# A two-layer streaming encoder: Newton's iteration for the Delta net's norms in three parts, and the input's norm in program order, scaled by parts

## The chip, the cores and the metric

The kernel runs on one core of one Trainium2 chip. The metric is device time in microseconds (us) of one execution; the time before is 2560.07 us, the median of 3 runs (2559.36 to 2560.88). The core's engines run side by side, each through its own list of instructions in order: TensorE (PE, matmuls and transposes), VectorE (DVE), ScalarE (ACT), GpSimd (POOL) and SyncE (SP, which issues most transfers). They wait for each other by semaphores.

## The reference

An input `x` of 1024 positions by 1024 channels goes through a layer of gated Delta net (linear attention by chunks), a gated FFN with a short convolution, a layer of banded softmax attention, a second FFN and a final norm. All of it is in float32. What the change touches is the first layer and the norm in front of it:

```python
def rmsnorm(x, g):
    y = xf * lax.rsqrt(jnp.mean(xf * xf, axis=-1, keepdims=True) + EPS)
    return (y * g.astype(jnp.float32)).astype(x.dtype)

def _l2norm(t):
    return t * lax.rsqrt(jnp.sum(t * t, axis=-1, keepdims=True) + EPS)

def gated_deltanet(xn, ...):
    proj = xn @ w_in
    qkv = silu(causal_dwconv(proj[..., :A_CONV_WIDTH], conv_w))      # 4 taps
    q = _l2norm(q heads) * A_HEAD_K ** -0.5      # 8 heads of 128
    k = _l2norm(k heads)
    ...
    o = chunk_gated_delta_rule(q, k, v, beta, g)
    o = rmsnorm(o, out_norm_w) * silu(z)
    return o @ w_out
```

So there are three reciprocal square roots in this stage: the input's norm over 1024 channels, the norms of q and k over 128, and the norm of the output over 128.

## The kernel before, in words

**Matmuls.** A float32 product is made from three passes in a faster 32-bit format: each operand is cut into a high half (ACT rounds it) and a low half (the difference, on DVE or POOL), and high x high, low x high and high x low are added in PSUM (`dense`, L113, its three matmuls at L119 to L121). Activations are `xh` and `xl` (8 k tiles of 128 channels, two halves `s` of 512 positions); a weight tile of 128 columns is cut by `split_w` (L91) into `whi` (ACT, L102) and `wlo` (POOL, L104, in four pieces).

**The start** (`begin_input`, L1227). Eight tiles of `x`, 128 positions each, are loaded (`take_x`), and two weight tiles, in this order on SP's queue: x tiles 0 to 3, the two weight tiles, x tiles 4 to 7. `norm_x` (L1150) makes for each x tile the sum of squares (ACT, L1154), its root (ACT, L1155), the reciprocal (DVE, L1156) and the scaling of the tile's 1024 channels in place (DVE, L1157). `turn_x` (L1159) transposes for each k tile four x tiles on TensorE into one PSUM tile `pxt` (L1163), from which ACT makes `xh` (L1164) and DVE `xl` (L1165). Three k tiles of the first half are turned, then the first projection tile begins, one k tile at a time, with the next transposes between. In this part only PE's order is written out by hand; on the other engines the framework's scheduler orders the instructions. Everything under `tc.manual_schedule(engines=...)` keeps, on those engines, the order in which the program records it.

**The Delta net stage.** Here PE, DVE and ACT are all recorded by hand, by a planner (`Flow`, L199). It holds generators, each with a rank and a lock (one item of a lock at a time), and a model time `T`. `wv.on("D", c)` books `c` us on its model of DVE and returns the time at which the work will be done; a generator that yields a time is taken up again half a microsecond (`slack`) after it, and one that yields nothing is taken up again after half a microsecond from the present. Between items the planner records one k tile's three matmuls of the dense stream (projections of q, k, v and z, later the output projection), 0.69 us of its time each. What it records stands in that order on PE, DVE and ACT; POOL and SP follow the scheduler. Among its items:

- `project` (L667): the convolution's taps on DVE (L682, L686), read from the PSUM tile `acc`, which is free again only then; SiLU on ACT (L691) and POOL (L692, L693).
- `gram(t)` (L738), four times, for four heads and half of the positions: the decay mask (L752), the Gram matrix on PE (L778), the norms' sums and the masked matrix on DVE (L783 to L790); at the end one `rsqrt` for all four heads, and the mark `scale`, for which `prep` waits. All calls of `gram` share a lock, so the next starts when one has ended.
- `invert_blocks` (L852): a solve of blocks of 16 on DVE, column by column (L869, L870).
- `merge` and `chain` (L891, L979): the triangular inverse, and the recurrence over chunks, in small matmuls on PE (L912 to L953; L993, L997, L1006), each of which waits for a short operation of DVE or ACT (L995, L1002, L1012).
- `finish(t, j)` (L1020), eight times, for two heads: the output's and q's norms in one factor by `rsqrt`, a scaling on POOL (L1043), and transposes.
- `yz`, `turn_last` (L1107, L1093): the gate, and the activations of the output projection (L1125, L1130); `out_tile` (L1311) is the output projection itself.

`rsqrt` (L604) is a reciprocal square root by bits on DVE: a shift and a subtraction for a first value (L607, L608), then three times Newton's step in three instructions (L610 to L612), 11 instructions on 16 or 8 numbers per partition.

Of the kernel before, what the change touches and what calls it, by code (L numbers as in the profile page):

```python
# [13 lines left out]
ALU = mybir.AluOpType  # L14
AX = mybir.AxisListType

P = 128
SEQ = 1024
# [10 lines left out]
def trunk_kernel(  # L29
# [15 lines left out]
    nc = tc.nc  # L45
# [394 lines left out]
    wv = None  # L440
# [130 lines left out]
    with ExitStack() as ph:  # L571
# [19 lines left out]
        def gt(name):  # L591
            return dp.tile([P, 8, 8], F32, name=name, tag=name)

        beta, gg, t1, t2 = gt("beta"), gt("gg"), gt("t1"), gt("t2")
# [9 lines left out]
        def rsqrt(y, a, w):  # L604

            yi = y.bitcast(I32)
            nc.vector.tensor_scalar(yi, a.bitcast(I32), 1, None, op0=ALU.logical_shift_right)  # L607
            nc.vector.tensor_scalar(yi, yi, -1, 0x5F3759DF, op0=ALU.mult, op1=ALU.add)  # L608
            for _ in range(3):
                nc.vector.tensor_tensor(w, y, y, op=ALU.mult)  # L610
                nc.vector.scalar_tensor_tensor(w, w, -0.5, a, op0=ALU.mult, op1=ALU.mult)
                nc.vector.scalar_tensor_tensor(y, w, 1.5, y, op0=ALU.add, op1=ALU.mult)  # L612

        ssk, ssq, sk, ck, nck = gt("ssk"), gt("ssq"), gt("sk"), gt("ck"), gt("nck")
        soo, ff, rr = gg, gt("ff"), gt("rr")
# [18 lines left out]
        def raw_tile(c0):  # L634
            raw = wp.tile([P, KT, P], F32, name="wraw", tag="wraw", bufs=2)
            nc.sync.dma_start(out=raw, in_=a_w_in[:, c0 : c0 + P].rearrange("(k p) m -> p k m", p=P))
            return raw
# [69 lines left out]
        def cs(c):  # L707
            return slice(c * P, (c + 1) * P)
# [3 lines left out]
        def heads(t):  # L712

            return t // 2, range(4 * (t % 2), 4 * (t % 2) + 4)
# [23 lines left out]
        def gram(t):  # L738

            s, hds = heads(t)  # L740
            Es, fetched = [], []
            sl = slice(4 * s, 4 * s + 4)
            h4 = slice(hds[0], hds[0] + 4)

            def fetch(hd):
                fetched.append(wv.T)
                Es.append(dq.tile([P, 4, P], F32, name="E", tag="E", bufs=3))
                nc.sync.dma_start(out=Es[-1], in_=d_g[sl, hd, :].rearrange("(o c) t -> o c t", o=1).broadcast_to([P, 4, P]))

            def decay(i):  # L750
                hd, E = hds[i], Es[i]
                nc.vector.tensor_tensor(E, E, negm.rearrange("p (o t) -> p o t", o=1).broadcast_to([P, 4, P]), op=ALU.add)  # L752
                yield wv.on("D", 0.8) - wv.slack
                for c in range(4):
                    nc.scalar.activation(E[:, c], E[:, c], AF.Exp, bias=ngc[:, 4 * s + c, hd : hd + 1])
                nc.sync.dma_start(out=d_e[hd][s], in_=E)
                stored[hd, s] = wv.T + 5.0
                yield wv.on("A", 1.45)

            fetch(hds[0])  # L760
            fetch(hds[1])
            yield wv.T + 5.5
            for i, hd in enumerate(hds):
                need = [("k", hd, 0) if s == 0 else ("in", hd)]
                if t > 1:
                    need.append(("merged", hd, s - 1))
                need = wv.when(*need)
                while need() is None:
                    yield wv.T + 0.5
                yield need()  # L770
                if i < 2:
                    fetch(hds[i + 2])
                yield from decay(i)
                slot = yield from wv.bank()
                pg = paux.tile([P, 4, P], F32, name="pg", tag="pa")
                kq, E = kqs[hd, s], Es[i]
                for c in range(4):
                    mm(pg[:, c], kq[:, 0, cs(c)], kq[:, 0, cs(c)], start=True, stop=True)  # L778
                wv.pe(4)
                h1 = slice(hd, hd + 1)  # L780
                mn = dq.tile([P, 4, P], F32, name="mn", tag="mn", bufs=8)
                for c in range(4):
                    nc.vector.tensor_tensor_reduce(out=mn[:, c], in0=pg[:, c], in1=ident, op0=ALU.mult, op1=ALU.add, scale=1.0, scalar=0.0, accum_out=ssk[:, 4 * s + c, h1])  # L783
                nc.vector.tensor_scalar(ssk[:, sl, h1], ssk[:, sl, h1], EPS, None, op0=ALU.add)
                nc.vector.reciprocal(t1[:, sl, h1], ssk[:, sl, h1])
                nc.vector.tensor_tensor(ck[:, sl, h1], t1[:, sl, h1], beta[:, sl, h1], op=ALU.mult)
                nc.vector.tensor_scalar(nck[:, sl, h1], ck[:, sl, h1], -1.0, None, op0=ALU.mult)
                wv.on("D", 1.95)
                for c in range(4):
                    nc.vector.scalar_tensor_tensor(mn[:, c], pg[:, c], nck[:, 4 * s + c, h1], E[:, c], op0=ALU.mult, op1=ALU.mult)  # L790
                slot[0] = t_ = wv.on("D", 1.2)
                yield t_ - wv.slack
                cm = dq.tile([P, 4, 32], F32, name="cm", tag="cm", bufs=2)
                for b in range(4):
                    r = slice(32 * b, 32 * b + 32)
                    nc.gpsimd.tensor_copy(cm[r], mn[r, :, r])
                nc.sync.dma_start(out=d_ms[t][i].rearrange("c b j i -> (b j) c i"), in_=cm)
                mns[hd, s] = mn
                wv.mark(("gram", hd, s), wv.on("G", 1.2, t_) + 2.5)
                yield max(wv.T + 0.5, fetched[min(i + 1, 3)] + 5.5)  # L800
            rsqrt(sk[:, sl, h4], ssk[:, sl, h4], t2[:, sl, h4])
            nc.vector.tensor_tensor(sk[:, sl, h4], sk[:, sl, h4], ssk[:, sl, h4], op=ALU.mult)
            wv.mark(("scale", t), wv.on("D", 3.5))

        def prep(hd, s):

# [213 lines left out]
        def finish(t, j):  # L1020

            s, hds = heads(t)
            hds = hds[2 * j : 2 * j + 2]
            sl = slice(4 * s, 4 * s + 4)
            h2 = slice(hds[0], hds[0] + 2)
            vvs = [parts[hd, s][2] for hd in hds]
            for hd, vv in zip(hds, vvs):
                junk = dp.tile([P, P], F32, name="junk2", tag="junk", bufs=1)
                for c in range(4):
                    nc.scalar.activation(junk, vv[:, c], AF.Square, accum_out=soo[:, 4 * s + c, hd : hd + 1])  # L1030
                t_ = wv.on("A", 1.9)
                yield
            yield t_ - wv.slack
            f = ff[:, sl, h2]
            nc.vector.tensor_scalar(f, ssq[:, sl, h2], EPS, 128.0 * EPS, op0=ALU.add, op1=ALU.mult)
            nc.vector.scalar_tensor_tensor(f, soo[:, sl, h2], 1.0 / 128.0, f, op0=ALU.mult, op1=ALU.add)
            r = rr[:, sl, h2]
            rsqrt(r, f, t2[:, sl, h2])
            t_ = wv.on("D", 3.6)
            yield t_ - wv.slack  # L1040
            for hd, vv in zip(hds, vvs):
                fa = rr[:, sl, hd : hd + 1].broadcast_to([P, 4, P])
                nc.gpsimd.tensor_tensor(vv, vv, fa, op=ALU.mult)  # L1043
                t_ = wv.on("G", 1.1, t_)
            yield t_
            for hd, vv in zip(hds, vvs):
                yield from (turn if t < 3 else turn_last)(hd, s, vv)
# [96 lines left out]
        def take_x(i):  # L1144

            t_ = dp.tile([P, 2, HALF + 4], F32, name="xt", tag="kq", bufs=8)
            x_tiles.append(t_.rearrange("p j t -> p (j t)")[:, 0:SEQ])
            nc.sync.dma_start(out=x_tiles[i], in_=x[i * P : (i + 1) * P, :])

        def norm_x(i):  # L1150
            t_ = x_tiles[i]
            jk = dp.tile([P, 8, P], F32, name="xj", tag="U", bufs=2).rearrange("p c t -> p (c t)")
            r = dp.tile([P, 2], F32, name="rsx", tag="rsx", bufs=4)
            nc.scalar.activation(jk, t_, AF.Square, accum_out=r[:, 0:1])  # L1154
            nc.scalar.activation(r[:, 1:2], r[:, 0:1], AF.Sqrt, scale=1.0 / SEQ, bias=epst)  # L1155
            nc.vector.reciprocal(r[:, 1:2], r[:, 1:2])  # L1156
            nc.vector.tensor_scalar(t_, t_, r[:, 1:2], None, op0=ALU.mult)  # L1157

        def turn_x(s):  # L1159
            for k in range(KT):  # L1160
# [66 lines left out]
        def begin_input():  # L1227
# [2 lines left out]
            nc.scalar.activation(warm[:, 0:1], epst, AF.Sqrt)  # L1230
            for i in range(4):
                take_x(i)
            for i in range(4):
                norm_x(i)
            raws = [raw_tile(m * P) for m in (8, 9)]
            wts = [split_w(raws[0], [P, KT, P])]
            for i in range(4, 8):
# [116 lines left out]
        wv = Flow()  # L1354
# [664 lines left out]
    with ExitStack() as ph:  # L2019
# [102 lines left out]
        def attend(a, tp, kv, sc, oT, more, tail):  # L2122
# [63 lines left out]
            def end():  # L2186
                last()
                finish()
# [70 lines left out]
        wv = Weave()  # L2259
# [104 lines left out]
    ctx_f, _ = ffn(1, h, hp, normed, tails[0], d_r1, norm_out)  # L2364
# [58 lines left out]
```

## Time and profile before

| | before |
|---|---|
| median of 3 runs | 2560.07 us |
| profiled execution | 2559.29 us |
| its span, first to last instruction | 2557.6 us |
| granted TensorE clock, mean | 0.999 |
| TensorE busy | 2498.8 us (98%) |
| VectorE busy | 1858.0 us (73%) |
| ScalarE busy | 1415.2 us (55%) |
| GpSimd busy | 1464.4 us (57%) |

In rows of the timeline the columns are start, duration (both us), engine, line, operation, output and inputs, and how many instructions the row merges; in brackets stands the engine's idle time before it and what ended it. Durations of matmuls are modelled ends; the distance of their starts tells the pace. In rows of waits stand the waiting engine, tile and line, what it waited for, the total in us, how often, and the longest.

### The profile page before, as it was taken

To read this page: it belongs to the slowest core of one execution; us is meant where nothing else is said; L and a number is where in the kernel's file an instruction comes from. 1 tells how busy PE (TensorE), PEld (TensorE's weight loads), DVE (VectorE), ACT (ScalarE), POOL (GpSimd) and SP (SyncE) were. 2 spreads that over 40 slices of the span, in tenths; PEclk is the share of its full clock that TensorE was granted. 3 is DMA by queue.
4 is the path that set the end of the run, shared out by engine and by line. 5 is a ranking of instruction groups with operands and counts; after the bars stand their busy time and mean duration, and the time that the engine had idled before them with its cause. 6 is when DMAs were issued, how large, how long until landed. Compare 5 with 4: busy or idle time off the path is not lost.

```text
span 2557.6 us, 39388 instructions
## 1 busy us (share of the span) xinstructions
PE 2498.8 (98%) x13933; PEld 2065.6 (81%) x13933; DVE 1858.0 (73%) x3109; ACT 1415.2 (55%) x2736; POOL 1464.4 (57%) x1460
## 2 busy tenths in 40 slices
PE   7999999999999999999999999999999999999999
PEld 5878888888877888888778888888876788888877
DVE  4775775554688888888876666667488788888886
ACT  5444555464455655555556565556455655556554
POOL 3655553445347777777726444443433777777771
PEclk9999999999999999999999999999999999999999
DMA  4433445464337777777831211113332567677786
GB/s 128 138 106 117 125 128 153 144 190 148 104 87 146 147 145 154 155 148 159 197 131 54 66 52 57 44 51 101 100 102 79 136 143 152 142 154 154 154 183 212
DMA packets 320598, 325.15 MB, mean 127 GB/s; under 512 B 32912, under 2 KB 244624, under 8 KB 320400
## 3 DMA queue, kind: packets, MB, share of 16 engines
q1 hardware_dynamic: 289440, 219.33, 29.1%
q0 software_dynamic: 25920, 94.38, 20.8%
q10 hardware_dynamic: 5040, 8.91, 1.0%
q8 instruction: 110, 1.80, 0.3%
q14 instruction: 88, 0.72, 0.1%
HBM read 179.89 MB, written 142.67 MB: 126 GB/s over the span
## 4 chain that ended last, share of the span: by engine, by line
PE 56%; DVE 5%; POOL 4%; issue 3%; ACT 2%; DMA 0%; POOLq 0%; ACTq 0%; DVEq 0%
PE pu L1463 8%; PE pu L1461 8%; PE pu L1462 8%; PE pd L1463 4%; PE pd L1461 4%; PE pd L1462 4%; PE acc L119 3%; PE acc L120 3%; PE acc L121 3%; POOL ul L1428 2%; PE ptp L2139 2%; PE poT L2169 1%; PE sc L2111 1%; PE poT L2168 1%; PE acco L119 1%
## 5 line engine op out<-in xcount | busy, mean ns | idle before, releaser
L1428 POOL TENSOR_TENSOR ul<-r,uh 128x512 fp32r<-128x512 f32 x282 | 442.6, 1588 | 300.8 <-ACT uh L1449 286.6
L119 PE MATMUL acc<-xh,whi 128*128 128x512 f32 x896 | 373.0, 417 | 1.7 <-DVE kq L686 1.6
L120 PE MATMUL acc<-xl,whi 128*128 128x512 f32 x896 | 352.7, 394 | 1.9 <-POOL xl L421 0.9
L121 PE MATMUL acc<-xh,wlo 128*128 128x512 f32 x896 | 352.2, 393 | 1.1 <-POOL wlo L104 1.1
L1449 ACT CAST uh<-r 128x512 fp32r<-128x512 f32 x296 | 181.6, 623 | 215.8 <-DVE r L1428 162.2
L104 POOL TENSOR_TENSOR wlo<-wraw,whi 128x256 fp32r<-128x256 f32 (+2 forms) x206 | 171.2, 860 | 139.1 <-ACT whi L102 105.4
L1463 PE MATMUL pu<-xh,ul 128*128 128x512 f32 x552 | 215.5, 390 | 1.5 <-POOL ul L1428 1.4
L1461 PE MATMUL pu<-xh,uh 128*128 128x512 f32 x552 | 215.3, 390 | 1.5 <-DVE h L1329 0.9
L1462 PE MATMUL pu<-xl,uh 128*128 128x512 f32 x552 | 215.2, 390 | 1.3 <-POOL xl L421 1.3
L1786 ACT COPY stage<-pd 128x1024 f32<-128x1024 f32 x180 | 174.9, 1013 | 49.3 <-PE pd L1463 49.2
L121 PEld LDWEIGHTS acc<-xh,wlo 128*128 128x128 f32 x896 | 168.4, 188 | 38.9 <-POOL wlo L104 1.5
L120 PEld LDWEIGHTS acc<-xl,whi 128*128 128x128 f32 x896 | 169.7, 189 | 25.9 <-POOL xl L421 3.0
L119 PEld LDWEIGHTS acc<-xh,whi 128*128 128x128 f32 x896 | 169.3, 189 | 24.3 <-DVE kq L686 2.0
L2119 POOL TENSOR_SCALAR sS<-sS,st 128x640 f32<-128x640 f32 (+4 forms) x128 | 86.6, 679 | 175.8 <-DVE st L2118 124.0
L1556 DVE SCALAR_TENSOR_TENSOR val<-vpre,colt,val 128x1023 f32<-128x1023 f32 (+2 forms) x92 | 151.6, 1647 | 40.6 <-ACT val L1553 40.5
L1428 POOL TENSOR_TENSOR dl<-a,dh 128x512 fp32r<-128x512 f32 x90 | 155.0, 1722 | 38.5 <-ACT dh L1449 38.5
L1556 DVE SCALAR_TENSOR_TENSOR gate<-gpre,colt,gate 128x1023 f32<-128x1023 f32 (+2 forms) x92 | 174.2, 1893 | 0.8
L1428 DVE TENSOR_TENSOR r<-r,r 128x512 f32<-128x512 f32 x168 | 134.8, 802 | 29.4 <-POOL ul L1428 27.9
L2117 ACT ACTIVATE sS<-sS,st 128x640 f32<-128x640 f32 (+4 forms) x128 | 89.3, 698 | 101.2 <-DVE st L2116 99.8
L1463 PEld LDWEIGHTS pu<-xh,ul 128*128 128x128 f32 x552 | 103.6, 188 | 25.3 <-POOL ul L1428 4.0
L1462 PEld LDWEIGHTS pu<-xl,uh 128*128 128x128 f32 x552 | 103.6, 188 | 24.2 <-POOL xl L421 2.9
L1461 PEld LDWEIGHTS pu<-xh,uh 128*128 128x128 f32 x552 | 103.6, 188 | 23.4 <-issue 1.3
(404 smaller groups left out, 7134.5 us busy)
## 6 DMA issues: line engine op xcount, KB each, us to landing
r<-in_f_w_up_dram SPq DMA_DIRECT2D x176, 256.0 KB, 4.4
d_r<-stage POOLq DMA_DIRECT2D x78, 512.0 KB, 7.8
d_c<-stage POOLq DMA_DIRECT2D x70, 512.0 KB, 7.9
a<-in_f_w_down_dram SPq DMA_DIRECT2D x72, 256.0 KB, 2.8
wraw<-in_a_w_in_dram SPq DMA_DIRECT2D x32, 512.0 KB, 4.4
d_e<-stage POOLq DMA_DIRECT2D x32, 512.0 KB, 8.8
wraw<-in_a_w_out_dram SPq DMA_DIRECT2D x16, 512.0 KB, 4.2
d_r<-h ACTq DMA_DIRECT2D x32, 256.0 KB, 3.5
```

Source lines behind the costliest of these rows:

```text
L104: nc.gpsimd.tensor_tensor(lo[:, c], raw[:, c], hi[:, c].bitcast(F32), op=ALU.subtract)
L119: mm(ps, hi[:, kw, wcol : wcol + P], rh[k][s], start=st, stop=False)
L120: mm(ps, hi[:, kw, wcol : wcol + P], rl[k][s], start=False, stop=False)
L121: mm(ps, lo[:, kw, wcol : wcol + P], rh[k][s], start=False, stop=sp)
L1428: tt = lambda eng, o, a, b, op: eng.tensor_tensor(o, a, b, op=op)
L1449: copy(hi, src)
L1461: mm(ps, w[0][:, cw], x[0], start=first, stop=False, skip_group_check=True)
L1462: mm(ps, w[0][:, cw], x[1], start=False, stop=False, skip_group_check=True)
L1463: mm(ps, w[1][:, cw], x[0], start=False, stop=last, skip_group_check=True)
L1556: nc.vector.scalar_tensor_tensor(t_[:, a:c1], p_[:, a - step : c1 - step], w[:, 2 - step : 3 - step], t_[:, a:c1], op0=ALU.mult, op1=ALU.add)
L1786: nc.scalar.copy(t_, ps)
L2117: nc.scalar.activation(S, S, AF.Exp, bias=st[:, 1:2], accum_out=st[:, 2:3])
```

## The change

`rsqrt` becomes a generator: after the first and the second of Newton's three steps it books 1.1 us of DVE time with the planner and yields. Both callers pass that on (`yield from`), and book less behind it: 1.3 us instead of 3.5 in `gram`, 1.1 instead of 3.6 in `finish`. In `begin_input` the norm of the first four x tiles is recorded under a manual schedule of DVE and ACT, and `norm_x` scales these four in two instructions, channels 0 to 383 and 384 to 1023, instead of one. What is computed is the same.

```diff
-            for _ in range(3):
+            for i in range(3):
                 nc.vector.tensor_tensor(w, y, y, op=ALU.mult)
                 nc.vector.scalar_tensor_tensor(w, w, -0.5, a, op0=ALU.mult, op1=ALU.mult)
                 nc.vector.scalar_tensor_tensor(y, w, 1.5, y, op0=ALU.add, op1=ALU.mult)
+                if i < 2:
+                    wv.on("D", 1.1)
+                    yield
...
-            rsqrt(sk[:, sl, h4], ssk[:, sl, h4], t2[:, sl, h4])
+            yield from rsqrt(sk[:, sl, h4], ssk[:, sl, h4], t2[:, sl, h4])
             nc.vector.tensor_tensor(sk[:, sl, h4], sk[:, sl, h4], ssk[:, sl, h4], op=ALU.mult)
-            wv.mark(("scale", t), wv.on("D", 3.5))
+            wv.mark(("scale", t), wv.on("D", 1.3))
...
-            rsqrt(r, f, t2[:, sl, h2])
-            t_ = wv.on("D", 3.6)
+            yield from rsqrt(r, f, t2[:, sl, h2])
+            t_ = wv.on("D", 1.1)
             yield t_ - wv.slack
...
-            nc.vector.tensor_scalar(t_, t_, r[:, 1:2], None, op0=ALU.mult)
+            for c in (slice(0, 3 * P), slice(3 * P, SEQ)) if i < 4 else (slice(0, SEQ),):
+                nc.vector.tensor_scalar(t_[:, c], t_[:, c], r[:, 1:2], None, op0=ALU.mult)
...
-            for i in range(4):
-                norm_x(i)
+            with tc.manual_schedule(engines={mybir.EngineType.DVE, mybir.EngineType.Activation}):
+                for i in range(4):
+                    norm_x(i)
```

## The prediction

> **What bounds the kernel.** I read the page first, then busy time by stretch, then TensorE's waits, then each engine's timeline over the first 32 us.
>
> ```profile
> PE 2498.8 (98%) x13933; PEld 2065.6 (81%) x13933; DVE 1858.0 (73%) x3109; ACT 1415.2 (55%) x2736; POOL 1464.4 (57%) x1460
> PE   7999999999999999999999999999999999999999
> ```
>
> TensorE (PE) is the bound: 98% busy, and only the first slice is visibly open. Work taken off VectorE (DVE) is worth nothing unless it ends a wait of PE. The Newton edits act between about 40 and 560 us; there the busy time by stretch (start:end, length, then PE, weight loads, DVE, ScalarE (ACT), GpSimd (POOL)) shows where PE stood idle:
>
> ```profile
> 120.00:160.00 40.00, 37.62 (x174) 30.68 (x173) 37.07 (x86) 16.30 (x42) 22.29 (x31) 1.00 0.33 96
> 280.00:320.00 40.00, 37.78 (x201) 30.68 (x204) 31.67 (x93) 22.52 (x75) 22.46 (x30) 1.00 0.45 126
> 320.00:480.00 160.00, 160.00 (x1783) 137.27 (x1777) 93.26 (x291) 86.91 (x279) 69.01 (x103) 1.00 0.49 142
> 480.00:540.00 60.00, 59.62 (x643) 50.46 (x643) 32.85 (x94) 33.17 (x88) 25.35 (x30) 1.00 0.56 170
> 540.00:560.00 20.00, 17.37 (x262) 15.64 (x248) 12.80 (x26) 14.68 (x37) 6.60 (x8) 1.00 0.63 197
> ```
>
> Idle PE time is 2.38 + 2.22 + 0.38 + 2.63 = 7.6 us, and none in 160 us of the middle. That is all that a better order of the Delta net stage can win. TensorE's waits from 40 to 600 us name it (in total, times, longest):
>
> ```profile
> PE pc L993 <- DVE S L1012: 2.0, 2, 1.6
> PE pq L721 <- POOL kq L693: 1.9, 2, 1.3
> PE acc L119 <- DVE kq L686: 1.6, 1, 1.6
> PE acc L121 <- POOL wlo L104: 1.1, 1, 1.1
> PE pm L948 <- ACT xh L1125: 0.8, 1, 0.8
> ```
>
> **Part 1: Newton's iteration in three parts.** It runs 12 times: 4 times for a group of heads in `gram`, 8 times for a pair in `finish`. The arithmetic is unchanged, 11 small instructions each. A member by its row:
>
> ```profile
> L612 DVE SCALAR_TENSOR_TENSOR sk<-t,sk x12: 174/176/1157, 122.8 to 473.2; 128x16 f32<-128x16 f32 x12
> ```
>
> At the median 0.18 us, 11 of them are 1.9 us, more where one takes 1.16 us. DVE has room for that on average, so the instructions themselves price at nothing: the cover is the dense matmuls that PE has meanwhile, and without cover a whole iteration would cost those 1.9 us.
>
> What changes is the plan. Each new `yield` hands the turn back, so other items and dense matmuls are recorded between. In the built order five of the 12 iterations still stand unbroken on DVE (nothing else was ready); seven are split. The knock-on is larger than the split: of TensorE's 12501 instructions 2150 change place, all between its 539th and about its 3490th. None is added or removed. The interruptions of the dense stream by small matmuls rise from 217 to 230. Does an interruption cost anything? Dense matmuls stand 0.23 us apart; two interruptions of 8 and of 4 small matmuls:
>
> ```profile
> 101.64 0.40 PE L121 MATMUL acc<-xh,wlo 128*128 128x512 f32 x1
> 101.88 1.05 PE L778 MATMUL pg<-kq 128*128 128x128 f32 x8
> 103.00 0.39 PE L120 MATMUL acc<-xl,whi 128*128 128x512 f32 x1
> ...
> 107.35 0.39 PE L121 MATMUL acc<-xh,wlo 128*128 128x512 f32 x1
> 107.58 0.60 PE L721 MATMUL pq<-ident,kq 128*128 128x128 f32 x4
> 108.25 0.39 PE L120 MATMUL acc<-xl,whi 128*128 128x512 f32 x1
> ```
>
> From the last dense matmul to the second one behind it is 1.36 and 0.90 us; less two dense spacings (0.46), 0.90 and 0.44: exactly 0.11 us per small matmul, nothing for the interruption. So 13 more are free, and TensorE's work in this stage is the same.
>
> The five waits, then, one by one in the new order. The wait of L121 for `wlo` (1.1): the 16 DVE instructions of one head's Gram step stood ahead of the convolution taps that lead to it; now they come after the block solve. I take it as gone. The wait of L119 (1.6) is for a PSUM bank that the taps on `kq` must free: between two sets of taps stood six solve columns, a mask add and a `finish` iteration; now four columns and the iteration. Gone. L948 (0.8) and the longer wait of L993 (1.6): there 64 small matmuls of the chain stood in a row behind dense matmul 1536, as no dense work was left before the output projection; in the new order none stand at that place, dense matmuls lie between them. Gone. The first wait of L721 keeps its neighbours: the same unbroken iteration, then the same taps. It stays, and so do the rest.
>
> Four waits are 1.1 + 1.6 + 0.8 + 1.6 = 5.1 us. But moved work is late somewhere else: one Gram step now lies 48 dense matmuls (11 us) later, and DVE, 37.07 us busy of 40 there, has no slack to choose from. A wait that a new order makes can't be read from the old trace. Bounds: all 7.6 us go (-7.6), or the old waits come back in other places with two more of the longest kind, 1.6 us (+3.2). I take half of the four waits as given back: -2.5 us, nearest to the stretches of 120 and 160 us where an order of this planner leaves about none to 2.4 us.
>
> **Part 2: the input's norm in program order.** ACT's first instructions now (order of the built program; `Sq` a square of an x tile, `Rt` its root, `W` a cast of a weight tile, `xh` the high half of a turned k tile): Sq0, W0, Rt0, Sq1, W1, Rt1, Sq2, Rt2, Sq3, Sq4, Rt3, Rt4, Sq5, xh0-xh2, a gate copy, Rt5, Sq6, xh3, xh4, Rt6, Sq7, xh5, xh6, Rt7, xh7. Only squares and roots are held in program order; the two weight casts were put between them. Before, both casts stood behind all four roots. ACT before:
>
> ```profile
> 5.13 1.06 ACT L1154 ACTIVATE xj<-xt 128x1024 f32<-128x1024 f32 x1 [1.90 <-DMA xt<-in_x_dram]
> 11.98 0.46 ACT L1155 ACTIVATE rsx<-rsx,epst 128x1 f32<-128x1 f32 x2
> 12.69 1.05 ACT L102 CAST whi<-wraw 128x1024 fp32r<-128x1024 f32 x1 [0.25 <-DMA wraw<-in_a_w_in_dram]
> 14.46 1.05 ACT L102 CAST whi<-wraw 128x1024 fp32r<-128x1024 f32 x1 [0.72 <-DMA wraw<-in_a_w_in_dram]
> 15.41 1.84 ACT L1164 ACTIVATE xh<-pxt,colt 128x512 fp32r<-128x512 f32 x3
> ...
> 23.66 1.06 ACT L1154 ACTIVATE xj<-xt 128x1024 f32<-128x1024 f32 x1
> 24.70 0.69 ACT L1164 ACTIVATE xh<-pxt,colt 128x512 fp32r<-128x512 f32 x1
> 25.27 0.30 ACT L1155 ACTIVATE rsx<-rsx,epst 128x1 f32<-128x1 f32 x1
> 25.46 1.06 ACT L1154 ACTIVATE xj<-xt 128x1024 f32<-128x1024 f32 x1
> 26.64 0.30 ACT L1155 ACTIVATE rsx<-rsx,epst 128x1 f32<-128x1 f32 x1
> ```
>
> The added wait: W0 waits for weights that land at about 12.7, and Rt0 and everything else stand behind it. The order of loads on SP's queue is the same, so the landing is too; POOL's order is the same. Steps from these rows: cast to next 0.95 (14.46 to 15.41), root to square 0.19, square to another operation 1.04, square to its own root 1.18. So W0 12.69, Rt0 13.64, Sq1 13.83, W1 14.87 (its weights are there by 14.46), Rt1 15.82, Sq2 16.01, Rt2 17.19, Sq3 17.38, Sq4 18.42, Rt3 19.46, Rt4 19.60, Sq5 19.8, xh0 20.84.
>
> DVE and PE before:
>
> ```profile
> 12.29 0.16 DVE L1156 RECIPROCAL rsx<-rsx 128x1 f32<-128x1 f32 x1 [1.34 <-ACT rsx L1155]
> 13.16 0.15 DVE L1156 RECIPROCAL rsx<-rsx 128x1 f32<-128x1 f32 x1
> 13.35 0.76 DVE L1157 TENSOR_SCALAR xt<-xt,rsx 128x1024 f32<-128x1024 f32 x1
> 16.13 2.07 DVE L1165 SCALAR_TENSOR_TENSOR xl<-pxt,colt,xh 128x512 fp32r<-128x512 f32 x3 [2.02 <-ACT xh L1164]
> ...
> 14.16 2.18 PE L1163 MATMUL pxt<-ident,xt 128*128 128x128 f32 x9 [0.39 <-DVE xt L1157]
> 16.15 0.79 PE L119 MATMUL acc<-xh,whi 128*128 128x512 f32 x1
> 20.07 0.60 PE L1163 MATMUL pxt<-ident,xt 128*128 128x128 f32 x4
> 26.80 0.40 PE L119 MATMUL acc<-xh,whi 128*128 128x512 f32 x1
> ```
>
> Reciprocal 0.31 behind its root (11.98 to 12.29): the fourth at 19.77, its first scale at 19.97. The scale of 384 channels, by elements between 0.16 (one element) and 0.76 (1024), is some 0.38 us: done at 20.35, against 14.11. So the fourth tile's first transpose starts at 20.4 instead of 14.16: +6.2 us. Scaling by parts saves 0.4 us here, already counted; with the three early tiles, the first parts let PE turn k0 to k2 at once. The second parts (0.16 + 0.60 x 640/1024 = 0.53) run beside those transposes; without that cover they would cost 0.5. Five extra DVE issues at 0.16 lie in the same idle.
>
> How much comes back? Before, the first tile of dense matmuls, with the remaining transposes between, ran from 16.15 to 26.80, held at the ends by xl. Now it starts after nine transposes, at 22.3. Lower bound of its end, by DVE alone: xl0 at 21.7 behind scale 4, then eight xl at 0.66 and three reciprocals with scales at 0.87, 29.6, and the last three matmuls 0.7: 30.3, +3.5 us. With PE's old pace of 10.65 us: 22.3 + 10.65 = 32.95, +6.2. The old pace holds about 1.2 us of waits for xh and xl that earlier squares now spare: 31.8. I take +5.0 us, nearer to PE's row, since PE's first matmuls are slow each time. From there PE is busy without a gap for 80 us, and nothing hides the shift.
>
> The row: nine transposes take 2.18 us at 14.16, and four take 0.60 at 20.07, half as long each, while the granted clock in the rows is 1.00. [...]
>
> **Sum.** +5.0 - 2.5 = +2.5 us. The profiled execution took 2559.29 (span 2557.6 and 1.7 around it), so 2561.8; it lies 0.8 under the median of 2560.07, on which the forecast is 2562.6. A measurement of this kernel tells about 0.2%, 5.1 us, from no change.
>
> **Rivals.**
> - The split does nothing for PE (D): five iterations are unbroken, DVE's time was not the limit, and as many waits appear as go. +5.0 alone: 2565.1, on the border to slower. For it: the unchanged neighbours of L721's wait. Against it: the 64 matmuls in a row are dispersed.
> - A worse order (B): more than 7.6 us of waits, as DVE in the first solve (37.07 of 40) gets Gram step and taps bunched again. +6.2 (PE's old pace) and +3.2 give 2569.5; with the middle values 2567. It decides from the point where new waits exceed those that go.
> - Faster (C): one mechanism, the start's loss is absorbed. If PE were held by xl alone with its first matmuls fast (+3.5) and every wait of the stage went (-7.6), 2556.0; below 2554.9 only if the weights land some 1.1 us earlier than 12.7. Against it: the landing follows four x tiles on a queue whose order is unchanged.
>
> **How the numbers follow.** Forecast 0.42; D 0.24 (half of it over the border); B 0.25; C 0.09. Slower 0.25 + 0.12 + 0.03 from the forecast's edge = 0.40; faster 0.08, as C can end just inside; same 0.52. The range leaves out 1 in 10 on either side: 2557.5 (start +4, three quarters of the idle gone) to 2568.5 (start +5.5, three more waits).
>
> **What would show it.** Right: ACT's first cast before its first root, idle from 6.3 to 12.7; the fourth tile's transpose near 20.4 and the second dense tile at 31 to 32; TensorE's waits of 1.1, 1.6 and the pair near 550 us gone; PE busy time unchanged. Wrong: the casts' weights land earlier, or PE idle between 120 and 560 us well away from 5 us.

## The result, and the profile after

The changed kernel takes 2569.42 us, the median of 7 runs (2567.3 to 2569.75); the kernel before took 2560.88 beside it (2558.84 to 2563.16). The ratio is 1.0029, with a 95% interval of 1.0020 to 1.0038: slower by some 7.4 us. The profiled execution took 2569.61, its span is 2567.9, 10.3 more than before.

The engines on the page of the changed kernel, busy time and number of instructions:

```profile
PE 2500.0 (97%) x13933; PEld 2068.6 (81%) x13933; DVE 1862.5 (73%) x3113; ACT 1415.7 (55%) x2736; POOL 1462.9 (57%) x1460
```

PE's work is the same to 1.2 us, so the 10.3 us are idle time and a slower clock. One row of the timeline cuts the loss in two: the first matmul of the first FFN, behind the whole Delta net stage. In the kernel before it starts at 665.38, in the changed kernel at 675.44:

```profile
675.44 0.47 PE L1466 MATMUL pu<-xh,uh 128*128 128x512 f32 x1 [0.88 <-DVE h L1334]
```

So 10.06 us of the 10.3 are lost by then. From there on the two traces run side by side.

**The start.** The timeline of the changed kernel, ScalarE and then TensorE:

```profile
5.17 1.06 ACT L1157 ACTIVATE xj<-xt 128x1024 f32<-128x1024 f32 x1 [1.94 <-DMA xt<-in_x_dram]
12.79 1.04 ACT L102 CAST whi<-wraw 128x1024 fp32r<-128x1024 f32 x1 [6.47 <-DMA wraw<-in_a_w_in_dram]
13.74 0.29 ACT L1158 ACTIVATE rsx<-rsx,epst 128x1 f32<-128x1 f32 x1
...
20.81 2.18 PE L1167 MATMUL pxt<-ident,xt 128*128 128x128 f32 x9 [1.27 <-DVE xt L1161]
22.64 0.78 PE L119 MATMUL acc<-xh,whi 128*128 128x512 f32 x1
24.77 0.78 PE L119 MATMUL acc<-xh,whi 128*128 128x512 f32 x1
26.70 0.48 PE L119 MATMUL acc<-xh,whi 128*128 128x512 f32 x1
33.06 0.39 PE L119 MATMUL acc<-xh,whi 128*128 128x512 f32 x1
```

ScalarE stands still from 6.3 to 12.8 us in front of the first cast, with one of the first four squares done. The fourth tile's transposes begin at 20.81 (14.16 before), the second dense tile at 33.06 (26.80): +6.3 us, and nothing hides it.

**The Delta net stage.** Busy time by stretch in the changed kernel (start:end, length, PE, weight loads, DVE, ACT, POOL, then the granted clock, DMA share, GB/s):

```profile
120.00:160.00 40.00, 38.72 (x183) 32.01 (x182) 34.88 (x94) 16.26 (x42) 22.79 (x31) 1.00 0.33 91
160.00:280.00 120.00, 115.38 (x1037) 97.30 (x1036) 68.18 (x170) 53.20 (x134) 63.87 (x90) 0.97 0.45 121
280.00:320.00 40.00, 39.40 (x195) 32.76 (x194) 34.62 (x92) 22.62 (x72) 23.27 (x30) 1.00 0.36 104
320.00:480.00 160.00, 156.88 (x1766) 135.09 (x1765) 97.32 (x310) 88.92 (x286) 72.38 (x110) 1.00 0.49 140
540.00:560.00 20.00, 19.81 (x327) 16.99 (x326) 11.43 (x23) 14.74 (x37) 9.57 (x12) 1.00 0.59 175
```

Of the stretches that were open, two are nearly shut (280 to 320, 540 to 560) and one is half shut (120 to 160, 1.3 us left of 2.4), and two that were full are open: 160 to 280 by 4.6 us, 320 to 480 by 3.1. With 0.03 from 480 to 540 the idle time is 9.8 us, against 7.6. TensorE's waits in the changed kernel from 40 to 600 us (total, times, longest):

```profile
PE pm L915 <- DVE T L911: 6.8, 2, 4.6
PE pq L724 <- POOL kq L696: 1.3, 1, 1.3
PE pv L848 <- DVE at L839: 0.9, 1, 0.9
```

The waits for `wlo`, on L119, L948 and the long one of L993 are gone. In their place `merge` (L915) waits twice for `T`, the transpose of the solved blocks, 4.6 and 2.2 us. Around the longer one the timeline of the changed kernel reads:

```profile
158.94 0.50 ACT L877 ACTIVATE W<-B,odd 128x256 f32<-128x256 f32 x1
...
160.60 0.37 SPq L751 DMA_DIRECT2D E<-d_g  x1
161.07 0.45 SPq L639 DMA_DIRECT2D wraw<-in_a_w_in_dram  x1
162.19 0.33 SPq L699 DMA_DIRECT2D d_kq<-u  x1
163.20 1.40 SPq L800 DMA_DIRECT2D d_m<-cm  x1
164.65 0.95 SPq L878 DMA_DIRECT2D d_u<-W  x1
170.50 0.91 SPq L901 DMA_DIRECT2D D<-d_u  x2
...
173.81 0.45 DVE L911 STREAM_TRANSPOSE T<-D 128x256 f32<-128x256 f32 x1 [4.66 <-DMA D<-d_u]
...
174.31 1.07 PE L915 MATMUL pm<-T,mn 32*32 32x32 f32 x64 [4.62 <-DVE T L911]
```

and in the kernel before:

```profile
157.53 0.49 ACT L874 ACTIVATE W<-B,odd 128x256 f32<-128x256 f32 x1
...
158.05 0.33 SPq L875 DMA_DIRECT2D d_u<-W  x1
161.10 0.91 SPq L898 DMA_DIRECT2D D<-d_u  x2
```

The solved blocks `W` are ready at 159.44 (158.94 + 0.50), but their store `d_u` is issued at 164.65, 5.2 us later; before it was 0.03 us. Ahead of it on SP stand the issues of the Gram step that the split moved forward: the load of its decays `E`, and its store `d_m`. Both wait themselves. By SP's waits from 150 to 166 us the load of `E` stood 11.9 us for VectorE's `mn` (L793), whose last row ends 1.1 us after `W` is ready; `d_m` stood 0.7 us until GpSimd's copies (L799) ended and took 1.4 to issue. Everything behind them in SP's list stood too. Then the store takes until 170.5 to be read back, 5.9 us; before, 3.05. Both delays together are 8.0 us. The second wait is of the same kind: `W` is ready at 317.8, and its store is issued at 321.96 behind two stores `d_y`, the first of which took 1.3 us to issue, and a load of weights, which stood 1.4 us for GpSimd.

What follows the wait is a second cost. Busy time by stretch of the changed kernel, columns as above:

```profile
174.00:180.00 6.00, 5.69 (x140) 4.82 (x141) 5.04 (x17) 1.00 (x2) 1.88 (x2) 0.50 0.55 173
180.00:184.00 4.00, 4.00 (x20) 3.31 (x20) 1.97 (x7) 0.01 (x1) 2.38 (x8) 0.99 0.76 159
```

After the gap the granted clock is 0.50 for six us. So the 10.06 us are 6.1 from the start (the 400th dense matmul, near 131 us, is 6.13 late) and 3.9 from the Delta net: 2.2 more idle time, and about 1.7 that is left for the matmuls at half clock. That rest is rough by half a microsecond: read directly, from the first matmul of L915 to the dense one behind L921, the same work took 5.30 us here and 3.15 in e2 (below), at full clock, so 2.15 more.

### The profile page after: what moved, and what is told of

Same layout as the page of the kernel before. It is cut to its first block, busy times and chain, and to the rows that moved or that the text cites. A ratio compares the mean times of both kernels' runs of the same rounds, so it can differ in the third digit from the quotient of the medians.

```text
span 2567.9 us, 39382 instructions
## 1 busy us (share of the span) xinstructions
PE 2500.0 (97%) x13933; PEld 2068.6 (81%) x13933; DVE 1862.5 (73%) x3113; ACT 1415.7 (55%) x2736; POOL 1462.9 (57%) x1460
## 4 chain that ended last, share of the span: by engine, by line
PE 52%; DVE 6%; POOL 4%; issue 4%; ACT 2%; DMA 1%; ACTq 0%; POOLq 0%; DVEq 0%
PE pu L1468 8%; PE pu L1467 8%; PE pu L1466 8%; PE pd L1468 3%; PE pd L1466 3%; PE pd L1467 3%; PE acc L119 3%; PE acc L120 3%; PE acc L121 3%; POOL ul L1433 2%; PE ptp L2144 2%; PE poT L2174 1%; PE sc L2116 1%; PE poT L2173 1%; PE acco L119 1%
## 5 line engine op out<-in xcount | busy, mean ns | idle before, releaser
L119 PE MATMUL acc<-xh,whi 128*128 128x512 f32 x896 | 374.3, 418 | 0.1
L119 PEld LDWEIGHTS acc<-xh,whi 128*128 128x128 f32 x896 | 169.7, 189 | 21.3 <-ACT xh L433 0.5
```

What stands on the lines that cost most here:

```text
L119: mm(ps, hi[:, kw, wcol : wcol + P], rh[k][s], start=st, stop=False)
```

## The experiments

Each kernel was timed beside runs of the kernel before. All compute the same. "FFN row" is the start of the row quoted above, less 665.38 of the profiled kernel before; it is free of what happens later and of the spread between executions of the later stages.

| kernel | median us | ratio to before (95%) | span less 2557.6 | FFN row |
|---|---|---|---|---|
| changed kernel | 2569.42 | 1.0029 (1.0020 to 1.0038) | +10.3 | +10.1 |
| e1 split alone | 2562.85 | 1.0004 (0.9995 to 1.0013) | +3.8 | +5.0 |
| e2 split, store on ACT | 2556.41 | 0.9981 (0.9972 to 0.9989) | -1.6 | -3.1 |
| e3 start alone | 2568.20 | 1.0027 (1.0017 to 1.0037) | +5.1 | +5.5 |
| e4 changed, store on ACT | 2561.29 | 1.0002 (0.9993 to 1.0010) | +1.7 | +1.4 |
| e5 scaling by parts alone | 2561.38 | 0.9999 (0.9988 to 1.0009) | +5.7 | +5.2 |
| e6 start, casts behind roots | 2565.18 | 1.0012 (1.0003 to 1.0021) | +5.4 | +2.8 |
| e7 before, store on ACT | 2562.95 | 1.0005 (0.9996 to 1.0014) | +4.6 | +3.9 |
| e8 all three | 2558.90 | 0.9990 (0.9981 to 0.9999) | -2.3 | -3.2 |
| e9 split, d_m on POOL | 2564.56 | 1.0013 (1.0004 to 1.0021) | +5.2 | +5.3 |
| e10 split in gram only | 2572.76 | 1.0043 (1.0030 to 1.0055) | +11.0 | +10.7 |
| e11 split in finish only | 2567.70 | 1.0025 (1.0016 to 1.0034) | +7.2 | +7.4 |
| e12 split, E load on ACT | 2561.02 | 1.0004 (0.9995 to 1.0013) | +2.3 | +1.5 |

The last two columns measure from one execution of before, which had no slow clock near 550 us and lies 1.8 us under the median of its runs beside e1. In e5 and e7 most of both columns is such a slow clock, in e6 some 2.3 of the FFN row's 2.8 (a further 2.6 of its span came behind that row); the last section takes it up.

**e1: the split alone.** The edits of `rsqrt` and its callers, and the start of the kernel before.

> Newton's split alone; the start is that of the kernel before. Theory Q (a queue): the split moves the Gram step ahead of the store of the solved blocks in SyncE's queue, so that the store is issued some 5 us and 4 us late, TensorE waits 4.6 and 2.2 us for the transposes T behind it, and runs at the slow clock after the longer wait. The four old waits of 5.1 us together go. Time: 3 to 4.5 us above the kernel before, some 1.5 us of it from matmuls at the slow clock. Rival R (the start changes everything): both new waits come from the start's shift in time; then they are absent here and the kernel is 2 to 4 us faster than before.

TensorE's waits in e1, first row:

```profile
PE pm L915 <- DVE T L911: 6.8, 2, 4.4
```

Both new waits are here without the new start, and the FFN row is 5.0 us late: theory Q, not R. In the changed kernel the split cost 3.9; it fits the difference that in e1 the clock is 0.50 for 3.4 us behind the second wait as well, and in the changed kernel it is not. The median is only 1.7 us up (the ratio says 1.0, with an interval that holds zero), less than the 3 to 4.5 expected. Most of the difference to the span's 3.8 lies in the kernel before: its profiled execution took 2559.29, its median here is 2561.13.

**e2 and e4: the store on the engine that ends the work.**

```diff
-                nc.sync.dma_start(out=d_u.rearrange(...), in_=W)
+                nc.scalar.dma_start(out=d_u.rearrange(...), in_=W)
```

> Newton's split alone, with the store of the solved blocks issued by ScalarE, which makes the last copy of them, instead of SyncE. Theory Q: the store leaves within 1 us of that copy, the waits for T are under 0.5 us each and no slow clock is granted between 160 and 280 us. Time: 2 to 4.5 us below the kernel before. Rival V (VectorE's order): T is late since the split puts other VectorE work ahead of it; then both waits stay within 1 us of their lengths and the time is that of the split alone, 3 to 4.5 us above.

> The changed kernel with the store of the solved blocks issued by ScalarE. Theory Q: the waits of 4.6 and 2.2 us and the slow matmuls behind them go, some 7 to 8.5 us: 1 to 3 us above the kernel before, which is the start's 6.1 less the four old waits. Rival V: nothing goes, 9 to 10 us above.

TensorE's waits in e2, and its row by stretch where e1 and the changed kernel have a granted clock of 0.91:

```profile
PE pm L915 <- DVE T L911: 1.3, 1, 1.3
```
```profile
160.00:200.00 40.00, 38.71 (x608) 31.33 (x607) 22.45 (x50) 19.77 (x46) 25.00 (x37) 1.00 0.50 140
```

PE, DVE and ACT keep their order; of four transfers only the queue changes. The FFN row moves from +5.0 to -3.1, 8.1 us (6.4 by the medians). Between the changed kernel and e4 it moves by 8.6, but 1.4 of that is there at the 400th dense matmul already, ahead of any such store, so the store's share is 7.2. Theory V, by which VectorE's order makes T late, is out. One wait of 1.3 us stays, longer than the 0.5 expected: `D` is loaded by SP, behind `d_m`. e4 comes to 1.4 us above by the FFN row, within the 1 to 3 expected, and to 0.5 by the ratio, below them. e2 beats both kernels, by 0.11 to 0.28% against the one before.

**e7: the control.** The same move in the kernel before.

> A control: the kernel before, with the store of the solved blocks issued by ScalarE instead of SyncE. Theory Q: in the kernel before this store leaves 0.03 and 1.3 us after its copy, so the move frees nothing there: -0.5 to +0.5 us. Rival G (any store taken off SyncE helps, with or without the split): 3 to 6 us below, as much as the same move gave beside the split.

Up to 445 us the dense matmuls are 0.3 us off the kernel before, and the time is not lower (1.0005). The move pays only where the split has put something ahead of the store.

**e9: d_m away from SP.** Split alone, with

```diff
-                nc.sync.dma_start(out=d_ms[t][i].rearrange("c b j i -> (b j) c i"), in_=cm)
+                nc.gpsimd.dma_start(out=d_ms[t][i].rearrange("c b j i -> (b j) c i"), in_=cm)
```

> Newton's split alone; the store of the solved blocks stays on SyncE, and the Gram step's store d_m, which stands right ahead of the first of them, is issued by GpSimd, which makes the copies that it waits for. Theory Q (what stands ahead in SyncE's queue holds the store back): the first new wait for T, 4.4 us at 168 us, falls under 1.5 us, and the slow clock behind it goes; the second, 2.3 us at 325 us, has a store of y and a weight load ahead of it and not d_m, and stays at 1.5 to 3 us: 4 to 6 us below the split alone, unless GpSimd, which now issues sixteen transfers of its own, becomes late itself. Rival A (it was not the queue, the store of the solved blocks merely gains by leaving from the engine that makes them): the first wait stays at 4 us or more, and the time is that of the split alone.

Here my theory in its first form fell. The store is issued at 156.28 instead of 158.48, 2.2 us earlier, but `D` can be loaded at 164.14 instead of 164.41, and the wait stays 4.4 us. The store now takes 7.8 us to land. So the place behind `d_m` was not what bounded the chain: whether the store is issued early or late, it lands at the same time, behind what was issued before it.

**e12: the load of E away from SP.** Split alone, with

```diff
-                nc.sync.dma_start(out=Es[-1], in_=d_g[sl, hd, :]...)
+                nc.scalar.dma_start(out=Es[-1], in_=d_g[sl, hd, :]...)
```

> Newton's split alone; all stores stay on SyncE, and the load of the Gram step's decays (E, 256 KB, some 6 us to land) is issued by ScalarE instead. The earlier runs left two delays of the store of the solved blocks: it is issued late behind other issues of SyncE, and it then takes 5.9 us to land where it took 3.0 in the kernel before. Theory L (it lands late since E, which moves slowly, and the loads behind it are served ahead of it in the same queue): with E on another queue the store lands within 4 us, the first wait for T falls from 4.4 to 1.5 to 3 us, 1 to 4 us below the split alone. Theory S (the transfers share the same engines and bytes, whatever queue they are on): the store still takes 5 us or more, the wait stays at 4 to 4.5 us, and the time is that of the split alone, or above it where ScalarE waits for a free E buffer.

The DMA issues from 152 to 166 us (queue, how many, KB each, median us from issue to landing), e1:

```profile
wraw<-in_a_w_in_dram SPq DMA_DIRECT2D x2, 512.0 KB, 6.9
E<-d_g SPq DMA_DIRECT2D x1, 256.0 KB, 6.8
d_u<-W SPq DMA_DIRECT2D x1, 256.0 KB, 5.9
D<-d_u SPq DMA_DIRECT2D x2, 64.0 KB, 2.2
```

and e12:

```profile
wraw<-in_a_w_in_dram SPq DMA_DIRECT2D x2, 512.0 KB, 4.5
d_u<-W SPq DMA_DIRECT2D x1, 256.0 KB, 2.1
E<-d_g ACTq DMA_DIRECT2D x1, 256.0 KB, 5.0
D<-d_u SPq DMA_DIRECT2D x2, 64.0 KB, 5.0
```

The row of the weights is the median of two loads: the one right behind `E` in e1 took 8.0 us, the one that e12 issues at 152.15, ahead of `E`, 4.2. The store takes 2.1 us instead of 5.9, and `D` is issued at 160.01 instead of 164.41. The longest wait falls from 4.4 to 2.1 us:

```profile
PE pm L915 <- DVE T L911: 4.1, 2, 2.1
```

These are the numbers of theory L, but only half of its reason is shown. ScalarE came to issue `E` at 159.76, when the store was all but landed, so `E` was out of the store's way in time as well as in place. In e2 it was so too: the store is issued at 153.21 and lands in 2.0 us, and `E` is issued at 154.38. No run has this store beside a moving `E` on the other queue. But `D`, issued on SP 0.25 us behind `E`, takes 5.0 us instead of 2.2, though `E` is on the other queue. The busy share of the DMA engines in tenths, 152 to 166 us in 40 slices of 0.35 us, e1 first and then e12, shows where they had room:

```profile
DMA  0000000000234260156789999999652110000038
DMA  0003546999300009909894000233333358997410
```

In e1 they are at 0 to 6 tenths from 155.5 to 158, while the first part of `E` moves and the weights stand behind it, and at 7 to 9 only from then on. In e12 they are at 2 or 3 tenths from 160.75 to 163.2, while `E` moves and `D` stands: of the 392 packets from 160 to 163 us 373 are of ScalarE's queue. So the store of e1 comes when the backlog behind `E` fills the engines, while `D` in e12 did not lack their time. What held `D` for 5.0 us, no run here shows. Ratios of e12 and e1 are the same, 1.0004, each against its own runs of the kernel before; by the profiled spans e12 is 1.5 us better, by the FFN row 3.5.

**e10 and e11: one call split at a time.** `gram` only, and `finish` only; the other call runs whole with its old due time.

> Newton's split in the Gram step's call alone; the call in the output's norm stays whole, at its old due time. In the program's order d_m stands right ahead of the first store of the solved blocks here, as with both calls split. Theory Q: the first wait for T of 4 to 5 us is there with granted clock under 0.95 from 160 to 200 us; 0 to 5 us above the kernel before. Rival F (the output norm's call makes the waits): no wait for T over 1 us, 1 to 4 us below.

> Newton's split in the output norm's call alone; the Gram step's call stays whole. In the program's order no d_m stands ahead of the first store of the solved blocks. Theory Q: no wait for T over 1 us near 168 us and the clock at 1.00 there; of the old waits of 5.1 us some go; 3 us below to 1 us above the kernel before. Rival F: the waits for T of 4 and 2 us are here, and it is 1 to 5 us above.

TensorE's waits, the first rows of e10:

```profile
PE pm L915 <- DVE T L911: 4.3, 1, 4.3
PE pc L1000 <- DVE vv L998: 2.4, 1, 2.4
```

and of e11:

```profile
PE pv L848 <- DMA vv<-d_v: 4.3, 2, 3.9
PE pq L724 <- POOL kq L696: 1.8, 2, 1.3
```

As to the place of the long wait the runs agree with Q (e10's granted clock is 0.50 for 6.8 us there, too): it is there when `gram` is split and not when `finish` is. As to the times both expectations missed. Either half costs more than the whole (FFN rows +10.7 and +7.4, against +5.0): each half gives the planner another order up to the end of the stage, with waits of its own, in e11 one of 3.9 us for a load of `vv`. The price of such an edit is not a sum over its calls. What makes the order of either half worse wasn't followed further.

**e3, e5 and e6: the start.** e3 is the new start alone. e5 has only the scaling in two parts; the planner keeps ScalarE's old order there. e6 has the new start with the order written by hand:

```diff
+            by_hand = lambda: tc.manual_schedule(engines={DVE, Activation})
+            with by_hand():
+                for i in range(4):
+                    norm_x(i)
+                wts = [split_w(raws[0], [P, KT, P])]
...
+                        for i in range(KT):
+                            dense(ps, wts[0], 0, xh, xl, FULL[i : i + 1], s, ...)
+                            next(it, None)
+                            if i == 0:
+                                wts.append(split_w(raws[1], [P, KT, P]))
+                            if 1 <= i <= 4:
+                                norm_x(i + 3)
```

> The start alone: norms of the first four tiles in program order with the scaling in two parts, Newton's iteration as before. Theory H (hoisted casts): the planner draws the casts of the first weight ahead of the roots, the transposes of the fourth tile begin at 20 to 21 us instead of 14.2, and the second dense tile at 33 instead of 26.8: 5.8 to 6.4 us above the kernel before, with the four old waits of Delta net there (7.6 us idle in all from 40 us on). Rival M (both parts lose and mix): the Delta net's waits of the changed kernel come from the start's shift; then they are here too, and it is 9 to 10 us above.

> The kernel before, with only the scaling of the first four tiles in two parts of the channels (384 and 640); the planner still orders ScalarE, and the casts of the first weight stay behind the four roots. Theory H (hoisted casts cost the start): scaling by parts alone moves the first dense tile by no more than 0.5 us either way, the fourth tile's first transpose begins at 13.6 to 14.2 us, and the time is that of the kernel before, -0.6 to +0.3 us. Rival P (the parts): eight scalings of VectorE in place of four hold back the tiles, the second dense tile is late by 3 to 6 us, and the time is 3 to 6 us above.

> The start alone, in program order and with the scaling in parts, but with ScalarE's and VectorE's order written by hand through the first dense tile: four squares and roots, then the first weight's casts, then the copies of the transposes. Newton's iteration as before. Theory H: the fourth tile's first transpose begins at 13 to 14 us and the second dense tile at 25.5 to 27, as in the kernel before: -2 to +0.5 us. Rival O (any hand order of the start costs, for norms of later tiles are bunched or PE starves in the second half): the second dense tile comes at 29 us or later and it is 3 us or more above.

e3: fourth tile at 20.68, second dense tile at 32.60 (+5.8), the four old waits back, the new ones absent; its time is 6.9 us up by the ratio (4.4 to 9.5), where 5.8 to 6.4 were expected. e5: 13.92 and 27.09 (+0.3); the parts are not what costs. e6, TensorE's timeline:

```profile
13.12 2.18 PE L1164 MATMUL pxt<-ident,xt 128*128 128x128 f32 x9 [0.89 <-DVE xt L1158]
...
23.25 0.50 PE L120 MATMUL acc<-xl,whi 128*128 128x512 f32 x1 [0.90 <-DVE xl L1166]
24.77 0.50 PE L120 MATMUL acc<-xl,whi 128*128 128x512 f32 x1 [0.56 <-DVE xl L1166]
26.87 0.50 PE L120 MATMUL acc<-xl,whi 128*128 128x512 f32 x1 [0.81 <-DVE xl L1166]
27.44 0.39 PE L119 MATMUL acc<-xh,whi 128*128 128x512 f32 x1
```

With the casts behind the roots the loss of 6 us is gone (theory H), and the fourth tile is even 1.0 us earlier than before. But there is no gain: the second dense tile is 0.6 late, as VectorE, which now does the norms of the later tiles between, makes PE wait 0.6 to 0.9 us three times for `xl`. The time, 3.1 us up by the ratio, is more than the start explains (0.5 us at the 400th dense matmul); the rest came behind 480 us.

**e8: split, store on ACT, and e6's start.**

> Newton's split, the store of the solved blocks on ScalarE, and the start with the casts behind the roots by hand. If the theories Q and H hold and the terms add: the store and the split take 4.7 us off and the start 0 to 2, so 4.5 to 6.5 us below the kernel before. If the gain of the split hangs on the time at which the Delta net begins, it is within 2 us of the kernel before.

2.6 us faster by the ratio where 4.5 to 6.5 were expected. The start by hand makes the 400th dense matmul 0.6 us late where I hoped for a gain; the FFN row is that of e2 (-3.2 and -3.1), the ratio 2.3 us behind it. e2 stays the best version.

## Where the prediction held, and where it failed

**Forecast.** 2562.6 us, +2.5: +5.0 for the start, -2.5 for the split. Measured +7.4 by the ratio, +10.3 in the profiled executions: on the median that the forecast started from, 2560.07 x 1.0029 = 2567.5, within the range and near its upper end of 2568.5; the median of 2569.42 itself is 0.9 above that end. What came is rival B, a worse order, with its mark: more idle time in the stage (9.8 us) than before (7.6). The sign of being wrong that I had set came with it, idle time from 120 to 560 us well away from 5 us. B's price of 2567 to 2569.5 fits, but in part by luck: its reason was VectorE bunched in the first solve, which e2 rules out for the long wait, it counted new waits at 1.6 us each, and it left out the clock. That the time fell within the range is luck of the same kind, for one of the two terms had the wrong sign.

**Part 1, the waits.** The four waits that I read out of the new order as gone are gone. PE's work is unchanged (2500.0 us busy against 2498.8), and 13 more interruptions of the dense stream cost nothing that shows. The step that failed is "half of the four waits as given back: -2.5 us". It stood on the sentence that a wait which a new order makes can't be read from the old trace. The Gram step's shift was in my own text, but I followed it on PE, DVE, ACT and POOL alone. SP's list in the built order had `d_m` right ahead of `d_u`, and the slow load of `E` ahead of both; with 5.8 us for `E`, the median in the views of the kernel before, and 0.03 us between `W` and its store in the old timeline, a wait of some 5 us could have been bounded. In place of -2.5 the split brought +3.9 in the changed kernel and +5.0 alone by the FFN rows (alone +1.0 by the ratio, -1.3 to +3.3). With the store out of the way it brought -3.1 (e2), so the gain that I looked for was there, and was spent in a queue: in a store issued 5.2 us late behind the Gram step's issues, and slow to land behind `E`.

**The bad bound of +3.2** for old waits that come back in other places assumed the longest old wait, 1.6 us, as the measure of a new one. The new ones were 4.6 and 2.2.

**What the bound also lacked** is the clock: after 4.6 us without work the granted clock was 0.50 for six us, some 2 us more. I had looked for slow matmuls at the start alone. A shorter gap came before a slow clock, too: in e12 the clock was 0.50 for 3.4 us behind a wait of 2.1.

**Part 2, the start.** The mechanism was right step by step: the cast ahead of the first root, ScalarE idle from 6.3 to 12.8, the fourth tile at 20.81 (20.4 forecast). The term was mis-sized: +5.0 against +6.3 here, +5.8 in e3, and it ended at my upper end, PE's old pace (32.95 forecast, 33.06 measured). I had taken 1.2 us off for waits that earlier squares spare. (The extra instructions of VectorE are four, not five: 3113 against 3109.) From the first to the second dense tile the changed kernel took 10.42 us, the kernel before 10.65. e4, with the same start, took 9.14. The difference lies in the clock. In e4 the rows of L119 fall from 0.78 to 0.48 at 24.13, 3.5 us behind the fourth tile; in the changed kernel at 26.70, 5.9 behind. The traces' clock records say the same: full clock is first granted at 20.04 in the kernel before, 23.62 in e4, 25.66 in e3 and 26.49 in the changed kernel; the 1.00 that the rows by stretch show ahead of that rests on no record. Behind the start of the fourth tile that is 5.9, 3.0, 5.0 and 5.7 us; what sets this length, no run shows. Nor does a run show the +5.5 that the range adds up for the start at its upper end, an estimate of mine: the price of the start was 4.8, 5.8 and 6.3 in the three executions of e4, e3 and the changed kernel. I took a middle where a range stood.

## What to carry to other kernels

Moving an item in a plan moves its DMAs too: follow each of them through the queue that issues it, and ask which store now stands behind a load that is slow or waits. A short store that somebody waits for belongs on the queue of the engine that ends the work, if that engine has time; here the one word was worth 8 us by the FFN row and 6 by the medians, and turned a loss into the best version, while in the kernel before, with nothing slow ahead of the store, it was worth nothing (e7). And a cast or copy that a scheduler may place freely is not harmless because it is short: while it waits for its transfer, its whole engine stands (here ScalarE, 6.47 us).

## What the runs showed of the hardware

**Transfers behind a slow load were slow too, though the DMA engines had room while it moved.** `E`, 256 KB read by a broadcast over partitions, took 6.8 us in e1, the weights right behind it 8.0 and the store 5.9; without it ahead they took 4.2 and 2.1 (e12). `D`, 64 KB, took 2.2 us in e1, issued when the store had landed, and 5.0 in e12, issued just behind `E` on the other queue, with the engines at 3 tenths or less for the first three of these 5 us.

**Short gaps came before a lower clock, in some executions.** Near 543 to 554 us the kernel before has three gaps close together: one within a group of equal matmuls (L929), ended by nothing that the profile shows, then the waits of L948 and L993. In its profiled execution the clock stayed at 1.00. In e5, whose code is the same from 40 us on, TensorE's timeline and the row by stretch read

```profile
543.40 0.28 PE L929 MATMUL pm<-T,mn 32*32 32x32 f32 x5
546.81 0.96 PE L929 MATMUL pm<-T,mn 32*32 32x32 f32 x27 [3.14 <-issue]
```
```profile
540.00:560.00 20.00, 16.86 (x230) 15.07 (x229) 9.97 (x22) 10.91 (x28) 5.78 (x7) 0.74 0.49 130
```

In e6 and e7 the gap within L929 was 0.7 and 0.8 us, and the clock of that stretch 0.92 and 0.87. The FFN row is late by 3 to 5 us in the three. The kernels with both calls split, in which these waits are gone, have 1.00 there. It fits that the times of single executions spread over 9.0 us for the kernel before (2557.9 to 2567.0 in the runs beside e5) and 9.5 for e5, but over 2.4 for e1, 2.5 for the changed kernel and 2.9 for e2; the other four with both calls split (e4, e8, e9, e12) are at 3.4 to 5.1. The spread goes with the clock: of the 100 executions of the kernel before beside the experiments, the 50 with a mean granted clock of 0.999 or more took 2557.9 to 2561.4 us, the 24 with 0.997 or less 2561.9 to 2567.0. That the gaps cause it is argued, and no run tested it alone.

A single gap came before it, too. A wait of 2.3 us in e1 (to 324.81), of 2.4 in e9 (to 324.59) and of 2.1 in e12 (to 165.97) was followed within 1.6 us by 3.4 us at clock 0.50, while one of 2.2 in the changed kernel (to 331.45) was followed by none. The stretches at 0.50 that the clock records show here inside the run lasted 3.41 us (from 1945.15 in the kernel before) or two or three times that (6.83 behind the long wait of the changed kernel, 10.24 in e5).

**The gap within L929** may go with the transfer of instructions. In the kernel before, a 16 KB packet of a DMA queue for instructions (q8) began at 539.90, and the gap ended at 543.57 with 0.20 us of idle time. In e5 that queue moved none from 536 to 544, while the other transfers kept the DMA engines 0.83 to 0.91 busy; its next packet began at 544.27, and PE went on at 546.81, 2.5 us later. In e6 and e7 it began at 542.38 and 542.11, and PE went on 2.3 us later in both. So PE seems to have waited for its instructions; that is an inference from four executions, and no run tested it.
